# A hybrid decoder layer on one core: three blocks' probabilities turned by DMA in place of four, and the fillers placed anew

## The chip, the core and the metric

The kernel runs on one core of a Trainium2 chip. Five engines work side by side, each through its own instructions in order: TensorE (PE, matrix products into PSUM banks), VectorE (DVE), ScalarE (ACT), GpSimd (POOL) and SyncE (SP), which issues most DMA transfers. They meet through semaphores only. The metric is the device time of one execution in microseconds (us): three timed runs of the kernel before gave 1909.85 us as their median, from 1906.83 to 1912.13.

## The reference, cut to what matters

```python
def reference(x, ...):                       # x: (1, 2048, 1024) float32
    h = rms_norm(x, attn_norm_g)
    z = h @ w_in                             # 1024 -> 2304: q 512, k 128, v 128, conv B, C, X 512 each
    q, k = rms_norm(q, q_norm_g), rms_norm(k, k_norm_g)        # per head of 64; 8 heads, 2 kv heads
    y_attn = swa_sink_attention(q, k, v, sinks)                # window 128, blocks of 128, a sink per head
    y_conv = gate_b * short_conv(gate_c * xc, conv_w)          # causal, depthwise, 3 taps
    y = concatenate([rms_norm(y_attn, attn_out_g), rms_norm(y_conv, conv_out_g)])
    x = x + y @ w_out
    hm = rms_norm(x, mlp_norm_g)
    return x + square(relu(hm @ w_up)) @ w_down                # 1024 -> 4096 -> 1024
```

All inputs and outputs are float32.

## The kernel before, in words

Every large product is made of three products of two float32r parts, a high part and the rest (`mm3`, lines 288 to 290: high times high, high times low, low times high), so the weights and activations are split on ACT (a cast) and DVE (a difference).

The work has three phases. The first, the mixers, goes over the sequence in four chunks of 512 rows (`c`, 0 to 3), each of four blocks of 128 rows (`b`, 0 to 15). The second and third are the two MLP products, made by a Strassen-like scheme of seven products each (lines 1538 and 1655). The change touches the mixers alone.

In a chunk PE has two kinds of work. The large one is a list of steps that a generator (`besides`) hands out: the conv projections of this chunk (`pc`, `px`, `pb`), the conv half of the output projection (`pout`), and q, k, v of the next chunk (`pz`); in the last chunk the transposes of the rows that the MLP will need (`pt_m`, `x_blocks`) are woven in. The small one is attention, block by block, and has long chains between its products on PE: the scores (`psc`, line 786), the softmax on DVE and ACT (`sc`, the exponentials at line 803, the final product at line 811), the probabilities turned, split and masked (`pp`), the product with the values (`po`, line 891), its rounding and squares (`o`, `at`), and the sum of squares (`pa`, line 912). `fill(n)` takes `n` steps of the large list between these points. `FILL[c]` holds the counts; they set how much PE work covers each chain. `PRIO`, `PRIO_Z` and `PRIO_P` shift the priorities by which the scheduler orders the instructions on each engine, so they decide who stands ahead of whom in a queue. The order on each engine is fixed when the program is built.

Two things are turned by DMA, not on PE. From block 4 on (`TURN_Q`), q and k of a block are normed (`qk_norm`), split into two 16-bit planes in the tile `sq`, and turned by a DMA transpose (line 742). For the blocks in `TURN_P` the same is done with the probabilities: `softmax` copies each half of `sc` into planes (`half`, line 819) and starts a transpose (line 820); `values` merges the planes into `pt` (line 392). All these tiles (`sq`, `half`, `pt`) are one buffer that they take in turn. So a half can be copied only when the half before it has landed, and the norm of the next block waits for both. Other blocks' probabilities are turned by eight PE transposes (`ptp`, line 839).

The rows of the next chunk are normed, turned and split by `prepare`, a generator of nine steps. `EARLIER` says at which steps of the second pair of conv projections the first five of them are taken.

Loads of weights that were split in chunk 0 and kept in DRAM are issued on SP (line 249), in one queue with the transposes, the raw rows and the stores. An SP instruction that waits holds up all behind it.

At the end of the conv half of the output projection, `pc` sums the squares; ACT (last chunk) or DVE copies them (`ms_c`), POOL makes the reciprocal root `rc`, and DVE's line 1044 needs it to empty the banks of `pout`, of which there are three.

Of the kernel before, what the change touches and what calls it, by code (L numbers as in the profile page):

```python
# [66 lines left out]
DOWN_BUFS = {"u": 2, "x1": 7}  # L67
UP_BUFS = {"w": 17, "u2": 3, "f11": 2, "u4": 2, "f12": 2, "s1": 1, "s2": 1, "s4": 1, "st": 5}
PC = (2, 0)
TURN_P = (6, 9, 13, 15)  # L70
TURN_Q = 4
PRIO_P = ((240, 0), (120, -30), (70, -80), (0, 120))
PRIO_Z = ((-50, -120, -180), (-250, 0, 430), (210, -230, 60), (0, -50, -150))
EARLIER = (6, 14, 31, 45, 46)

CHP = CH + 32
STEPS = 3
# [9 lines left out]

PRIO = ((210, 0, 0, -70, 30, 0, 20, -10, -160, 0, 0, 310, 0, 10), (160, -60, -60, -60, 40, 50, 140, 40, 0, -90, 0, 10, 0, -120), (0, 0, 70, -10, 40, 0, 200, -40, 0, -130, 260, 150, -170, -10), (200, 0, 210, 0, 30, 0, 0, 40, -10, 0, -40, 30, 60, -120), (160, 80, 0, 10, 0, 0, 20, -20, -20, 0, 0, 120, 0, 0))  # L90

FILL = (((18, 15), (9, 8, 7, 8, 5), (5, 5, 5, 12, 9), (1, 11, 5, 9, 7), (11, 10, 8, 2, 2)), ((25, 18), (6, 14, 13, 1, 0), (19, 10, 11, 2, 3), (13, 10, 15, 7, 9), (6, 14, 8, 8, 7)), ((21, 15), (5, 22, 7, 4, 1), (8, 2, 6, 1, 9), (24, 14, 16, 0, 1), (13, 14, 9, 5, 3)), ((30, 0), (6, 8, 1, 6, 7), (11, 7, 6, 13, 6), (1, 11, 4, 7, 8), (13, 7, 7, 0, 8)))

# [1 line left out]
def hymba_layer(  # L97
# [91 lines left out]
    def ahead(i):  # L189

        offset = PRIO[stage[0]][i]
        return tc.high_priority(offset=offset) if offset else nullcontext()


    def ahead_z(i):

        offset = PRIO_Z[stage[0]][i]
        return tc.high_priority(offset=offset) if offset else nullcontext()

    def ahead_p(i):  # L200

        offset = PRIO_P[stage[0]][i]
        return tc.high_priority(offset=offset) if offset else nullcontext()
# [479 lines left out]
    with tc.tile_pool(name="mix_small", bufs=1) as mix_small, tc.tile_pool(name="mix", bufs=1) as mix:  # L683
# [90 lines left out]
        def softmax(b, qt, sc):  # L774
# [36 lines left out]
            nc.vector.tensor_tensor(sc, sc, den[:, :, None].to_broadcast([P, HEADS, P]), op=ALU.mult)  # L811
            if b in TURN_P:
                with ahead_p(0):
# [9 lines left out]
        def values(b, zt, v_before, sc, n_fill, fill):  # L823
# [3 lines left out]
            def probabilities(kv):  # L827

                if b in TURN_P:
                    pt = mix.tile([P, nh, DH], F32, tag="sq", name=f"pt_{nm}_{kv}", bufs=1)  # L830
# [228 lines left out]
        def besides(c, before, h, yt, rc, x1, h_next, z_next):  # L1059
# [8 lines left out]
            for j in range(2):  # L1068
                for n, _ in enumerate(conv_pair(c, h, j, yt, ssc)):
                    if blocks and n % X_EVERY == 0:  # L1070
                        next(blocks, None)
                    if j and not blocks and n in EARLIER:
                        next(steps)
# [41 lines left out]
        def mixers(c, before, h, z):  # L1115


            last = c + 1 == NCHUNK
            n_fill = FILL[c]
            stage[0] = c  # L1120
# [574 lines left out]
```

## Time and profile before

| what | us |
|---|---|
| timed runs: median (lowest to highest) | 1909.85 (1906.83 to 1912.13) |
| the profiled execution's own time | 1914.36 |
| its span, first to last instruction | 1912.7 |
| mixers, until the first MLP product | 690.2 |
| MLP, first product | 609.6 |
| MLP, second product and the last stores | 612.9 |

PE is busy for 1894.5 us of the span, DVE 1235.9, ACT 878.6, POOL 290.1; the mean granted clock of PE is 0.998. A row of the timeline holds the start, the length, the engine, the line, the operation, the tiles (written <- read) and shapes; in brackets stands how long the engine was idle before it and what ended that. The ends of PE's matmuls are modelled, and successive matmuls overlap: how fast PE goes is read from the starts.

### The profile page before, as it was taken

What the parts mean: (1) busy time and instruction counts of PE and PEld (TensorE: products, weight loads), DVE (VectorE), ACT (ScalarE), POOL (GpSimd) and SP (SyncE); (2) the same over time, 40 slices, a digit from 0 to 9 for tenths busy, and PEclk for the clock granted to TensorE, in tenths of its full rate; (3) what the DMA queues carried; (4) which work ended last, traced back from release to release, by engine and by line L of the source; (5) the groups of instructions that cost most, each with busy time, mean ns of one, the idle gap of its engine ahead of it and who ended that gap; (6) DMA issues with size and microseconds to landing.
All of it is one profiled execution on the core that took longest, in us unless ns stands there. A gap on an engine that the chain in (4) does not pass through costs nothing.

```text
span 1912.7 us, 24444 instructions
## 1 busy us (share of the span) xinstructions
PE 1894.5 (99%) x8742; PEld 1574.3 (82%) x8742; DVE 1235.9 (65%) x1945; ACT 878.6 (46%) x1621; POOL 290.1 (15%) x477
## 2 busy tenths in 40 slices
PE   9999999999999999999999999999999999999999
PEld 8888888888887788888888888888888888888887
DVE  5886567658558859999787766666534334448541
ACT  6665356556545446545565545454332332232320
POOL 2222213213212212233111111111000000100000
PEclk9999999999999999999999999999999999999999
DMA  8988967667687888778576544448954456866631
GB/s 297 333 285 205 332 221 227 222 216 249 210 316 228 237 303 256 221 217 249 192 241 202 175 144 159 141 147 328 361 194 151 136 172 222 284 228 213 214 128 56
DMA packets 282138, 426.13 MB, mean 223 GB/s; under 512 B 101016, under 2 KB 185760, under 8 KB 269216
## 3 DMA queue, kind: packets, MB, share of 16 engines
q1 hardware_dynamic: 253184, 348.91, 56.7%
q0 software_dynamic: 15424, 51.40, 6.9%
q10 hardware_dynamic: 13408, 24.26, 3.4%
q8 instruction: 69, 1.13, 0.3%
q14 instruction: 53, 0.43, 0.1%
HBM read 286.35 MB, written 125.83 MB: 216 GB/s over the span
## 4 chain that ended last, share of the span: by engine, by line
PE 86%; DVE 5%; DMA 4%; ACT 2%; POOL 1%; issue 1%; SPq 0%; DVEq 0%; ACTq 0%; POOLq 0%
PE u L1538 32%; PE d L1655 32%; PE pout L288 2%; PE pout L289 2%; PE pout L290 2%; PE pz L289 1%; PE pz L290 1%; PE pz L288 1%; PE pz L601 1%; DMA sc_b<-half_b 1%; PE psc_b L786 1%; PE pc_c L289 1%; PE pc_c L288 1%; PE pc_c L290 1%; PE pb_c L288 1%; PE pb_c L290 1%
## 5 line engine op out<-in xcount | busy, mean ns | idle before, releaser
L1538 PE MATMUL u<-op_x,wop 128*128 128x512 f32 x2688 | 609.8, 389 | 0.0
L1655 PE MATMUL d<-op_w,op_f 128*128 128x512 f32 x2691 | 609.5, 389 | 0.0
L1655 PEld LDWEIGHTS d<-op_w,op_f 128*128 128x128 f32 x2691 | 505.0, 188 | 104.5
L1538 PEld LDWEIGHTS u<-op_x,wop 128*128 128x128 f32 x2688 | 504.5, 188 | 105.1 <-issue 0.6
L480 DVE TENSOR_TENSOR op_f<-op_f 128x1024 fp32r<-128x1024 f32 x112 | 137.0, 1225 | 238.4 <-ACT op_f L479 237.9
L479 ACT CAST op_f<-op_f 128x1024 fp32r<-128x1024 f32 x112 | 117.7, 1051 | 354.8 <-DMA op_f<-fop 342.8
L498 ACT CAST wop<-wu 128x512 fp32r<-128x512 f32 x156 | 96.4, 620 | 91.9 <-PE u L1538 89.5
L499 DVE TENSOR_TENSOR wop<-wu,wop 128x512 fp32r<-128x512 f32 x156 | 111.0, 713 | 32.6 <-ACT wop L498 20.0
L1274 POOL DMA_DIRECT2D fop<-s x96 | 52.1, 542 | 441.3 <-DVE s L1277 434.7
L1280 DVE TENSOR_TENSOR u<-u,u 128x512 f32<-128x512 f32 x128 | 87.9, 687 | 21.3 <-PE u L1538 21.2
L480 DVE TENSOR_TENSOR op_w<-raw,op_w 128x1024 fp32r<-128x1024 f32 x56 | 68.4, 1223 | 25.1 <-ACT op_w L479 24.8
L479 ACT CAST op_w<-raw 128x1024 fp32r<-128x1024 f32 x56 | 58.8, 1051 | 44.0 <-PE d L1655 21.7
L852 POOL TENSOR_SCALAR_AFFINE_SELECT pp_b<-pp_b 128x512 fp32r<-128x512 f32 x60 | 47.7, 805 | 144.1 <-ACT pp_b L845 100.2
L1286 ACT ACTIVATE u<-u 128x512 f32<-128x512 f32 x64 | 40.4, 632 | 53.0 <-DVE u L1280 50.8
L803 ACT ACTIVATE sc_b<-sc_b,ngm_b 128x128 f32<-128x128 f32 x128 | 49.7, 390 | 20.2 <-DVE ngm_b L800 20.1
L1487 POOL DMA_DIRECT2D wds<-raw x16 | 8.5, 533 | 330.0 <-DVE raw L1485 320.1
L498 ACT CAST wop<-wu_s 128x512 fp32r<-128x512 f32 x64 | 39.5, 619 | 31.0 <-PE u L1538 27.7
L499 DVE TENSOR_TENSOR wop<-wu_s,wop 128x512 fp32r<-128x512 f32 x64 | 46.0, 720 | 11.5 <-ACT wop L498 11.3
L288 PE MATMUL pout<-w_wo,yt_c 128*128 128x512 f32 x128 | 50.5, 395 | 1.6 <-DVE x L1044 1.6
L288 PE MATMUL pb_c<-h_a,w_wb 128*128 128x512 f32 x128 | 51.8, 405 | 0.0
L290 PE MATMUL pb_c<-h_a,w_wb 128*128 128x512 f32 x128 | 51.3, 401 | 0.0
L289 PE MATMUL pb_c<-h_a,w_wb 128*128 128x512 f32 x128 | 51.3, 401 | 0.0
(253 smaller groups left out, 3144.3 us busy)
## 6 DMA issues: line engine op xcount, KB each, us to landing
op_f<-fop SPq DMA_DIRECT2D x112, 512.0 KB, 4.3
raw<-in_w_down_dram SPq DMA_DIRECT2D x72, 512.0 KB, 4.4
wu<-in_w_up_dram SPq DMA_DIRECT2D x128, 256.0 KB, 4.0
w_wo<-wo SPq DMA_DIRECT2D x24, 1024.0 KB, 6.7
fop<-s POOLq DMA_DIRECT2D x96, 256.0 KB, 2.7
fop<-u ACTq DMA_DIRECT2D x64, 256.0 KB, 2.3
op_x<-xop SPq DMA_DIRECT2D x28, 512.0 KB, 6.8
w_q<-q SPq DMA_DIRECT2D x12, 1024.0 KB, 5.7
```

Of the source, the lines that this page charges most:

```text
L288: nc.tensor.matmul(ps, st(0), mv(0), start=first, stop=False)
L289: nc.tensor.matmul(ps, st(0), mv(1), start=False, stop=False)
L290: last_sum[0] = nc.tensor.matmul(ps, st(1), mv(0), start=False, stop=last).ins
L479: nc.scalar.copy(op[:, 0], raw)
L480: nc.vector.tensor_tensor(op[:, 1], raw, op[:, 0].bitcast(F32), op=ALU.subtract)
L498: splits.append(nc.scalar.copy(hi, blk).ins)
L499: lows.append(nc.vector.tensor_tensor(lo, blk, hi.bitcast(F32), op=ALU.subtract).ins)
L803: nc.scalar.activation(sc[:, hd, :], sc[:, hd, :], AF.Exp, bias=ngm[:, hd : hd + 1], accum_out=den[:, hd : hd + 1])
L1274: eng.dma_start(fop_dram[tb][ORDER_DOWN.index(i)][n // 2][:, n % 2], b)
L1280: return nc.vector.tensor_tensor(dst, ps, b, op=ALU.add).ins
L1538: nc.tensor.matmul(pt, wops[i][:, a, k, :], xops[tb, p][k // 2][:, b, k % 2, :], start=p not in GOES_ON and k + j == 0, stop=k + j == NB + ...
L1655: nc.tensor.matmul(ps[tb][j][:, cs], fs[tb][:, a, k, j * P : (j + 1) * P], w[:, b, k, cs], start=first and p not in GOES_ON and k + n == 0 ...
```

## The change

Five tables are replaced. `TURN_P` loses block 9, whose probabilities are then turned on PE. The others say where the fillers stand, who goes first in a queue, and when the rows of the next chunk are prepared. The MLP is not edited.

```diff
-TURN_P = (6, 9, 13, 15)
+TURN_P = (6, 13, 15)
 TURN_Q = 4
-PRIO_P = ((240, 0), (120, -30), (70, -80), (0, 120))
-PRIO_Z = ((-50, -120, -180), (-250, 0, 430), (210, -230, 60), (0, -50, -150))
-EARLIER = (6, 14, 31, 45, 46)
+PRIO_P = ((-270, -750), (690, 0), (0, 0), (180, -120))
+PRIO_Z = ((-80, -60, 510), (-230, 90, 0), (130, 0, 60), (0, 0, -100))
+EARLIER = (3, 11, 32, 33, 37)
...
-PRIO = (...)
+PRIO = (...)
-FILL = (((18, 15), (9, 8, 7, 8, 5), ...
+FILL = (((18, 13), (12, 8, 7, 8, 6), ...
...
```

What moves, at three places. The first is ACT's queue in the last chunk, between the softmax of block 13 and the norm of block 14 (`half_b13` are the planes, `xt_m` raw rows that are scaled, `o_b12` the output of block 12, `sq_b14` the norm). Before:

```order
L819 COPY half_b13_0_5613<-sc_b13_5482 128x512 x2
L866 CAST vz_632<-z3_1_4875 128x2x64
L866 CAST vd_633<-v_diff_635 128x2x64
L364 ACTIVATE xt_m0_3_6161<-xt_m0_3_6161,rs_x1_233 128x1024
L364 ACTIVATE xt_m1_3_6162<-xt_m1_3_6162,rs_x1_233 128x1024
L899 COPY o_b12_5806<-po_b12_0_5737 64x512
L819 COPY half_b13_1_5617<-sc_b13_5482 128x512 x2
L866 CAST vz_632<-z3_1_4875 128x2x64
L726 ACTIVATE sq_b14_5621<-z3_2_4876 128x640
L899 COPY o_b12_5806<-po_b12_1_5801 64x512
```

and now:

```order
L819 COPY half_b13_0_5635<-sc_b13_5509 128x512 x2
L364 ACTIVATE xt_m0_3_6157<-xt_m0_3_6157,rs_x1_233 128x1024
L364 ACTIVATE xt_m1_3_6158<-xt_m1_3_6158,rs_x1_233 128x1024
L866 CAST vz_632<-z3_1_4871 128x2x64
L899 COPY o_b12_5836<-po_b12_0_5783 64x512
L866 CAST vd_633<-v_diff_635 128x2x64
L819 COPY half_b13_1_5639<-sc_b13_5509 128x512 x2
L978 CAST yt_c3_0_0_5810<-y_c3_0_0_5675 128x512
L981 ACTIVATE ssc3_5393<-y_c3_0_0_5675 128x512
L866 CAST vz_632<-z3_1_4871 128x2x64
L726 ACTIVATE sq_b14_5643<-z3_2_4872 128x640
L899 COPY o_b12_5836<-po_b12_1_5831 64x512
```

The second half of block 13 still stands behind the two raw rows and behind `o_b12`, and two conv instructions come between it and the norm of block 14.

The second is SP's queue at the end of chunk 1, where the weights of the next chunk's q are loaded (`w_q12_1` is the last of four parts). Before:

```order
L820 DMA_TRANSPOSE sc_b6_2794<-half_b6_0_2912 128x8x128
L1080 DMA x1_1_3_3049<-in_x_dram 128x1024
L430 DMA_TRANSPOSE xt_a2_3_3032<-half_a2_3_0_3118 128x8x128
L430 DMA_TRANSPOSE xt_a2_3_3032<-half_a2_3_1_3119 128x8x128
L820 DMA_TRANSPOSE sc_b6_2794<-half_b6_1_2916 128x8x128
L249 DMA w_q12_1_3363<-q1_918 128x2048
```

and now:

```order
L820 DMA_TRANSPOSE sc_b6_2794<-half_b6_0_2909 128x8x128
L1080 DMA x1_1_3_3085<-in_x_dram 128x1024
L249 DMA w_q12_1_3363<-q1_918 128x2048
L820 DMA_TRANSPOSE sc_b6_2794<-half_b6_1_2913 128x8x128
L408 DMA xt_a3_0_4285<-in_x_dram 128x1024
L430 DMA_TRANSPOSE xt_a2_3_2992<-half_a2_3_0_3155 128x8x128
L430 DMA_TRANSPOSE xt_a2_3_2992<-half_a2_3_1_3156 128x8x128
```

The load has passed three transposes.

The third is ACT's queue near the end of the last chunk, around the copy of the conv squares (`ms_c3`). Before:

```order
L866 CAST vz_632<-z3_3_4877 128x2x64
L899 COPY o_b14_6471<-po_b14_0_6423 64x512
L819 COPY half_b15_1_6281<-sc_b15_6126 128x512
L1101 COPY ms_c3_6437<-pc3_6432 128x4
L819 COPY half_b15_1_6281<-sc_b15_6126 128x512
```

and now:

```order
L899 COPY o_b14_6452<-po_b14_0_6416 64x512
L866 CAST vz_632<-z3_3_4873 128x2x64
L866 CAST vd_633<-v_diff_635 128x2x64
L983 ACTIVATE y_c3_1_1_6192<-y_c3_1_1_6192 128x512
L1101 COPY ms_c3_6433<-pc3_6428 128x4
L866 CAST vz_632<-z3_3_4873 128x2x64
L819 COPY half_b15_1_6277<-sc_b15_6122 128x512 x2
```

The copy of the squares has passed the second half of block 15.

On PE the three points that the prediction uses are: between the scores of block 13 and those of block 14 there were 126 matmuls of 512 columns and 24 transposes, and there are 126 and 36; between the scores of block 15 and its second product with the values there were 159 matmuls of 512 columns, and there are 129; between the second and third group of block 3's scores there were three, and there are eight.

More of the change, by code (lines that the diff above doesn't have):

```diff
@@ L86 @@
 SOON = 330
-PRIO = ((210, 0, 0, -70, 30, 0, 20, -10, -160, 0, 0, 310, 0, 10), (160, -60, -60, -60, 40, 50, 140, 40, 0, -90, 0, 10, 0, -120), (0, 0, 70, -10, 40, 0, 200, -40, 0, -130, 260, 150, -170, -10), (200, 0, 210, 0, 30, 0, 0, 40, -10, 0, -40, 30, 60, -120), (160, 80, 0, 10, 0, 0, 20, -20, -20, 0, 0, 120, 0, 0))
-FILL = (((18, 15), (9, 8, 7, 8, 5), (5, 5, 5, 12, 9), (1, 11, 5, 9, 7), (11, 10, 8, 2, 2)), ((25, 18), (6, 14, 13, 1, 0), (19, 10, 11, 2, 3), (13, 10, 15, 7, 9), (6, 14, 8, 8, 7)), ((21, 15), (5, 22, 7, 4, 1), (8, 2, 6, 1, 9), (24, 14, 16, 0, 1), (13, 14, 9, 5, 3)), ((30, 0), (6, 8, 1, 6, 7), (11, 7, 6, 13, 6), (1, 11, 4, 7, 8), (13, 7, 7, 0, 8)))
+PRIO = ((370, 0, -150, -100, 30, 0, -30, -10, -160, 0, 0, 480, 400, 0), (170, -60, -90, -60, 30, 110, -70, 40, 0, -80, 0, 70, 60, -140), (0, 0, 20, -10, 40, 0, 90, -40, 10, -130, 160, 60, 50, 0), (200, 0, 190, 0, 30, 0, 50, 40, 80, -30, -10, 30, 50, -90), (160, 80, 0, 10, 0, 0, 20, -20, -20, 0, 0, 120, 0, 0))
+FILL = (((18, 13), (12, 8, 7, 8, 6), (4, 2, 5, 12, 9), (1, 10, 5, 9, 10), (11, 9, 9, 2, 2)), ((25, 17), (6, 14, 13, 1, 0), (20, 10, 7, 2, 3), (12, 10, 16, 6, 12), (5, 16, 8, 5, 5)), ((16, 19), (10, 18, 5, 0, 1), (8, 2, 6, 1, 9), (28, 15, 13, 0, 6), (13, 18, 7, 7, 1)), ((30, 2), (9, 8, 1, 7, 8), (11, 3, 8, 11, 2), (2, 13, 5, 2, 6), (13, 12, 2, 0, 2)))
 @with_exitstack
```

## The prediction

> **What bounds the kernel now.** I read the page's first line, then busy time by stage, then who TensorE (PE) waited for, and last the chain of waits around the longest wait. The columns of the stages are: stretch, its length, busy us (instructions) of PE, its weight loads, DVE, ACT, POOL, granted clock, DMA share, GB/s.
>
> ```profile
> span 1912.7 us, 24444 instructions
> ...
> 140.00:300.00 160.00, 156.94 (x774) 130.00 (x773) 102.83 (x214) 84.88 (x212) 38.03 (x61) 1.00 0.82 253
> 300.00:500.00 200.00, 197.91 (x979) 166.01 (x979) 139.09 (x301) 114.94 (x279) 50.78 (x75) 1.00 0.70 228
> 500.00:690.20 190.20, 182.43 (x902) 151.49 (x902) 130.75 (x259) 85.97 (x213) 43.28 (x66) 0.98 0.77 248
> 690.20:1299.80 609.60, 609.60 (x2690) 504.54 (x2689) 478.40 (x696) 331.38 (x543) 104.72 (x168) 1.00 0.62 203
> 1299.80:1912.70 612.90, 609.32 (x2692) 504.67 (x2690) 278.71 (x270) 174.64 (x174) 22.72 (x44) 1.00 0.60 206
> ```
>
> From 690.2 us on PE never waits before the final output, and the change edits nothing there. All it can win is PE's idle time before that: 3.1 + 2.1 + 7.8 = 13.0 us in the three stretches from 140 on, and whatever the clock loses (0.98 in the last stretch). The longest waits of PE (total, times, longest):
>
> ```profile
> PE pa_b L912 <- DVE o_b L907: 3.8, 1, 3.8
> PE pz L289 <- DMA w_q<-q: 2.0, 2, 1.0
> PE pt_m L370 <- DVE xt_m L371: 2.0, 2, 1.1
> ...
> PE pout L288 <- DVE x L1044: 1.6, 1, 1.6
> ...
> PE po_b L891 <- POOL pp_b L852: 0.8, 1, 0.8
> ...
> PE psc_b L786 <- DVE sc_b L797: 0.6, 1, 0.6
> ```
>
> **The change, part by part.**
>
> *Block 9's turn goes back to PE.* Eight 128x128 transposes are added; four ACT copies, four DVE copies and two DMA transposes go, all off the path. Such transposes among matmuls, from PE's timeline (start, length):
>
> ```profile
> 549.54 0.60 PE L370 MATMUL pt_m<-ident,xt_m 128*128 128x128 f32 x4
> 549.90 0.48 PE L288 MATMUL pc_c<-h_a,w_wc 128*128 128x512 f32 x1
> 550.22 0.39 PE L289 MATMUL pc_c<-h_a,w_wc 128*128 128x512 f32 x1
> 550.45 0.39 PE L290 MATMUL pc_c<-h_a,w_wc 128*128 128x512 f32 x1
> ```
>
> A matmul of 512 columns starts 0.23 us after the one before (550.45 - 550.22). From 549.54 to 550.22 are 0.68 us, less one such matmul 0.45 for four: 0.11 each, so **+0.9** for eight. With it goes the POOL wait of 0.8, which is block 9's second product behind its DMA-turned half; transposed on PE, the probabilities have 191 matmuls of 512 columns of cover ahead of them. **-0.8** (ends: 0 and -0.8).
>
> *A weight load passes three transposes in SP's queue* (chunk 1, before the projection of chunk 2). SP's queue by time:
>
> ```profile
> 304.56 1.23 SPq L820 DMA_TRANSPOSE sc_b<-half_b  x1
> ...
> 306.55 4.59 SPq L430 DMA_TRANSPOSE xt_a<-half_a  x2
> 311.23 1.26 SPq L820 DMA_TRANSPOSE sc_b<-half_b  x1
> 312.59 0.54 SPq L249 DMA_DIRECT2D w_q<-q  x1
> ```
>
> The load at 312.59 is the one that PE waits 1.0 for at about 318. It now stands right ahead of the L430 pair at 306.55, some 6 us earlier: **-1.0**. What it pushes back is row tile a2_3 and a half of block 6, whose product has 9 score matmuls (1.1 us) more of cover. Ends: 0, if the buffer and not the queue held the load, and -1.0. Chunk 0's equal wait keeps its queue order: 0.
>
> *Scores of block 3*: eight matmuls in place of three stand between its second and third score group, 1.1 us more against a wait of 0.6: **-0.6**.
>
> *The last chunk's raw rows.* pt_m waited twice for the one bank to be emptied by DVE. Its first pair has 22 matmuls between in place of 6, and DVE now empties it before its score copies; the second pair has 9 in place of 6, 0.7 us. Of 2.0 I take **-1.5** (ends 0, -2.0).
>
> *The long wait.* The chain of waits (start, us, what) that ends at pa_b of block 12:
>
> ```profile
> 567.89 6.39 DMA xt_m<-x_dram
> ...
> 574.36 1.15 ACT xt_m L364
> ...
> 576.02 1.15 ACT half_b L819 x2
> ...
> 577.18 4.77 DMA sc_b<-half_b
> ...
> 582.04 0.75 ACT sq_b L726
> ...
> 588.80 0.21 DVE o_b L907
> ```
>
> ACT turns to block 13's second half only after a raw row tile has come in; that half's transpose frees the buffer that the norm of block 14 needs, and block 12's o_b stands behind that norm on DVE. PE pays more than the wait:
>
> ```profile
> 558.11 2.08 PE L786 MATMUL psc_b<-kw,qt_b 128*128 128x256 f32 x16
> ...
> 589.15 0.56 PE L912 MATMUL pa_b<-mean,o_b 128*128 128x1 f32 x2 [3.83 <-DVE o_b L907]
> ...
> 590.57 0.63 PE L290 MATMUL pb_c<-h_a,w_wb 128*128 128x512 f32 x1
> 591.00 0.63 PE L288 MATMUL pb_c<-h_a,w_wb 128*128 128x512 f32 x1
> ...
> 594.84 0.47 PE L288 MATMUL pc_c<-h_a,w_wc 128*128 128x512 f32 x1
> ...
> 598.56 0.64 PE L786 MATMUL psc_b<-kw,qt_b 128*128 128x256 f32 x4
> ```
>
> After 3.83 us of idleness matmuls start 0.43 apart, not 0.23, until 594.84: 12 of them, 12 x 0.20 = 2.4 us. The 1.6 us wait later on cost the clock nothing (1.00 in this stretch):
>
> ```profile
> 640.00:660.00 20.00, 18.44 (x85) 15.01 (x84) 13.09 (x24) 7.78 (x17) 5.00 (x7) 1.00 0.98 268
> ```
>
> From block 13's scores (558.11) to block 14's (598.56) are 40.4 us; the order holds 16 score matmuls there, 126 of 512 columns and 24 transposes, 16 x 0.12 (2.08 for 16, with the last one's drain) + 126 x 0.23 + 24 x 0.11 = 33.5 at PE's pace. So PE is 6.9 late by block 14, whose scores in turn start the moment their operands are there.
>
> In the changed order 12 more transposes lie between the two (+1.3 us of cover), but ACT's half of block 13 now stands behind o_b of the same block 12 whose product comes 48 matmuls and 20 transposes after the scores, 48 x 0.23 + 20 x 0.11 = 13.2 us; with the product's own four matmuls and a 64-row and a 128-column copy ahead of it (an estimate: 1.8 us) the half starts some 15.0 us after the scores, which took 16 x 0.12 = 1.9 us: 576.02 - 560.0 = 16.0 before. The chain behind is the same. Lateness 6.9 - 1.3 - 1.0 = 4.6, so **-2.3**. Its parts fall on two waits, before pa_b and before block 14's scores, 2 to 3 us each. Ends: -6.9 (transpose at its shortest and better DVE order) and 0.
>
> The Trainium skill ("TensorE: Matmul & The Clock Gate", Part 1) says the array goes to half clock after an idle window of about 3.4 us, and that this window runs free. The 0.43 after 3.83 us agrees. By it, two waits of 2 to 3 us cost no clock, and the sum stays; one joined wait of 4.6 would add the 2.4 again.
>
> *The reciprocal root of the last conv norm.* ACT's copy L1101, from ACT's and DVE's timelines:
>
> ```profile
> 648.21 0.62 ACT L819 COPY half_b<-sc_b 128x512 uint16<-128x512 uint16 x1 [2.87 <-DMA sc_b<-half_b]
> 648.85 0.16 ACT L1101 COPY ms_c<-pc 128x4 f32<-128x4 f32 x1
> 650.51 2.07 DVE L1044 SCALAR_TENSOR_TENSOR x<-pout,rc,x 128x512 f32<-128x512 f32 x3 [0.52 <-POOL rc L185]
> ```
>
> L1101 queued behind block 15's second half, which waited for the first half's transpose. It now stands ahead of it. From the copy to the first emptied bank are 2.4 us (648.85 to 650.51 plus a third of 2.07), and 12 matmuls, 2.8 us, cover it: **-1.6** (ends 0, -1.6).
>
> *What is late next: block 15.* Its second product had 159 matmuls of 512 columns behind the scores and has 129, 6.8 us less. Its scores, its last operand, its first transpose, and the landing times of all eight transposes of the kind:
>
> ```profile
> 627.07 2.15 PE L786 MATMUL psc_b<-kw,qt_b 128*128 128x256 f32 x16
> ...
> 657.35 0.69 DVE L846 TENSOR_TENSOR pp_b<-pt_b,pp_b 128x512 fp32r<-128x512 f32 x1
> ...
> 639.81 8.37 DMA sc_b<-half_b
> ...
> DMA to landing us min/median/max: 2.7/2.9/8.4
> ```
>
> Here, with 8.37 for the first, the operand was there 658.0 - 629.1 = 29 us after the scores; 129 matmuls, 12 transposes and 6 short ones are some 31.4: 2.4 to spare. With 8.37 for the second too, in place of 2.9, it is 5.5 later, 3.1 short. I take **+1.0** between 0 and 3.1, for this and for smaller covers that shrank.
>
> Sum: 0.9 - 0.8 - 1.0 - 0.6 - 1.5 - 2.3 - 1.6 + 1.0 = **-5.9**. The profiled execution took 1914.36 us, 1.7 around its span; it becomes 1908.5. It is 4.5 above the median of the runs shown, 1909.85, so I set the difference against that: **1904**.
>
> **Rivals.**
>
> *A. The chain hides entirely.* If block 13's second transpose lands in the median 2.9 and not 4.77, 1.9 less; with DVE's better order (block 14's copy no longer behind a conv product, 1.5) the lateness is near 1. With block 15 safe too: 1904 - 3.4 - 1.0 = 1899.6. For it: half of the eight landed within 2.9. Against: ACT's half still sits behind a load.
>
> *B. The long wait belongs to the profiled execution.* That execution is 4.5 slower than the median; if late transfers made the 3.83 and the 1.6, the timed runs hold less to win: -5.9 + 2.3 + 1.6 leaves -2.0, 1908. Against: the waits of 0.6 to 1.1 are in queue order, not in lateness.
>
> *C. Late transposes decide.* The place is ACT in the last chunk, where both remaining DMA-turned blocks have their halves behind other work. At 8.37 in place of 4.77 block 13 is 3.6 later; the joined wait passes 3.8 and costs the clock 2.4; block 15 is short by 3.1, and its wait, between the 1.6 after which the clock stayed at 1.00 and the 3.83 that cost 2.4, adds 1.2. 1904 - 1.0 + 3.6 + 2.4 + 3.1 + 1.2 = 1913, slower than before. It decides from about 5 us of landing time for block 13 and 5.3 for block 15's second. For it: both blocks had a late one. Against: the one at 639.81 ran beside weight loads that are now issued in another order.
>
> *D. Nothing moves*, because each wait only shifts to the next consumer: 1909.85 + 0.9 = 1911.
>
> **How the numbers follow.** Forecast 1904: 0.36. A: 0.25. B: 0.18. C: 0.11. D: 0.10. What a measurement of this kernel can tell from no change is about 0.3%, 5.7 us: faster means under 1904.1. That takes half of the forecast and all of A, and a little of B: 0.46. Slower, above 1915.6, takes C's worse side and a tail of unforeseen waits: 0.10. Same: 0.44. The range 1895 to 1913 takes in A with its unknown ends (the many waits of 0.2 to 0.4 that I cost at nothing) and D, and reaches to C.
>
> **What would show it.** Right: the wait of pa_b under 3 us with the clock at 1.00 from 580 to 600; no w_q wait near 318; no wait of pout for L1044 near 650; PE's MLP start at 683 to 685 in place of 690.2. Wrong: a wait of po_b in the last chunk, block 14's scores waiting over 3 us, or PE idle again over 10 us after 140.

## The result and the profile after

The changed kernel takes 1915.63 us (median; 1912.38 to 1918.11) against 1910.65 (1906.44 to 1913.57) for the kernel before on the same chip. The ratio is 1.0026 [1.0018, 1.0034]: **5 us slower**, where 5.9 faster was forecast, and outside the range of 1895 to 1913.

The stages again, with the columns of before:

```profile
span 1913.5 us, 24453 instructions
...
140.00:300.00 160.00, 156.23 (x774) 129.77 (x773) 101.98 (x211) 84.45 (x207) 38.98 (x60) 1.00 0.80 253
300.00:500.00 200.00, 197.31 (x966) 165.10 (x965) 140.62 (x297) 113.62 (x279) 48.41 (x74) 0.99 0.70 228
500.00:690.20 190.20, 184.67 (x923) 153.46 (x923) 131.30 (x261) 87.44 (x215) 43.66 (x67) 0.99 0.77 246
690.20:1299.80 609.60, 609.60 (x2691) 504.55 (x2690) 477.87 (x696) 331.04 (x542) 105.03 (x168) 1.00 0.62 203
```

PE's idle time after 140 us is 3.8 + 2.7 + 5.5 = 12.0 us where it was 13.0. By this pair of profiles the kernels look alike: 1915.2 us in the profiled execution of the changed kernel, 1914.36 in that of the kernel before. But the first is at the median of its timed runs and the second 3.7 above its own. PE's waits in the changed kernel (total, times, longest):

```profile
PE pa_b L912 <- DVE vd L867: 4.1, 1, 4.1
PE pz L289 <- DMA w_q<-q: 1.8, 1, 1.8
...
PE po_b L891 <- DVE pp_b L846: 1.5, 2, 1.0
PE pc L1093 <- DVE ssc L984: 1.4, 1, 1.4
PE pa_b L912 <- DVE o_b L907: 1.2, 1, 1.2
PE psc_b L786 <- DVE kw L768: 0.9, 1, 0.9
PE pt_m L370 <- DVE xt_m L371: 0.5, 1, 0.5
```

Four waits of before have gone or shrunk as forecast: w_q near 318 us, block 3's scores, pt_m (2.0 to 0.5), pout for L1044 in the last chunk (1.6 to none). The long wait, of pa_b for block 12, is longer (3.8 to 4.1; its row names `vd`, the last instruction of DVE to end before it, but `pa_b` reads `o_b`, which was ready 0.15 us earlier). And three stand where nothing was forecast: pa_b of block 3 (1.2), pc of chunk 2 (1.4), and w_q between chunks 0 and 1, which was 1.0 and is 1.8. Two smaller ones were not forecast either: block 7's scores wait 0.9 for `kw`, and block 13's product with the values waits 1.0 in the last chunk, where it waited 0.4.

**Chunk by chunk over all profiles.** One profile of each kernel can't carry a difference of 5 us whose terms are 1 us each. The runs below built kernels that share whole chunks with one kernel or the other, so each chunk's order was profiled four to ten times. A stage ends with the first matmul of the q projection of the next chunk, so the stage called chunk 2's below also holds the end of chunk 1, from block 7's scores on. In the changed kernel these marks are, and the first MLP product behind them:

```profile
148.80 0.48 PE L288 MATMUL pz<-w_q,h_a 128*128 128x512 f32 x1
...
315.11 0.39 PE L288 MATMUL pz<-w_q,h_a 128*128 128x512 f32 x1
...
486.15 0.39 PE L288 MATMUL pz<-w_q,h_a 128*128 128x512 f32 x1
...
690.95 0.61 PE L1538 MATMUL u<-op_x,wop 128*128 128x512 f32 x2
```

| stage, us | order of before: mean (lowest to highest, profiles) | changed order | difference |
|---|---|---|---|
| to pz of chunk 1 | 147.9 (147.6 to 148.4, 10) | 148.7 (148.3 to 149.1, 6) | +0.8 |
| to pz of chunk 2 | 165.2 (164.0 to 167.2, 10) | 166.4 (165.7 to 167.6, 6) | +1.2 |
| to pz of chunk 3 | 166.8 (166.2 to 167.5, 9) | 170.2 (169.5 to 171.0, 5) | +3.4 |
| to the first MLP product | 205.3 (203.2 to 208.2, 6) | 206.0 (204.8 to 207.6, 4) | +0.7 |
| MLP, to PE's last matmul | 1219.4 (1218.8 to 1221.3, 12) | 1218.9 (1218.8 to 1219.1, 5) | -0.5 |

The sum, +5.6, agrees with the timed +5.0. The last two differences are smaller than the spread of the profiles, so they show nothing. Two things are seen that the one profile of before hid. The loss is in chunks 0 to 2, above all in chunk 2 (to pz of chunk 3). And the profile on which the prediction stood has the longest last chunk of its six, 208.2 us: nearly 3 us above their mean.

The +3.4 of chunk 2 can be taken apart over the same profiles. PE's idle time there rises by 1.0 us (mean 1.3 and 2.3). In three of the five changed profiles the granted clock is 0.5 for 3.4 us, in none of the nine before: 1.0 us on the mean. And PE makes 32 transposes there, not 20: eight are block 9's, and four are made here and no longer in the last chunk. At the 0.11 us each of the prediction that is 1.3 us, of which the four only moved.

### The profile page after: what moved, and what is told of

Read it like the earlier page. It is cut to its first block, busy times and chain, and to the rows that moved or that the text cites. A ratio compares the mean times of both kernels' runs of the same rounds, so it can differ in the third digit from the quotient of the medians.

```text
span 1913.5 us, 24453 instructions
## 1 busy us (share of the span) xinstructions
PE 1895.9 (99%) x8750; PEld 1574.7 (82%) x8750; DVE 1236.4 (65%) x1941; ACT 877.1 (46%) x1617; POOL 290.6 (15%) x477
## 4 chain that ended last, share of the span: by engine, by line
PE 89%; DVE 5%; DMA 3%; ACT 1%; issue 1%; POOL 0%; SPq 0%; DVEq 0%; ACTq 0%; POOLq 0%
PE u L1538 32%; PE d L1655 32%; PE pout L288 2%; PE pout L289 2%; PE pout L290 2%; PE pz L289 1%; PE pz L288 1%; PE pz L290 1%; PE pc_c L289 1%; PE pc_c L290 1%; PE pc_c L288 1%; PE px_c L290 1%; PE px_c L289 1%; PE px_c L288 1%; PE pz L601 1%; PE psc_b L786 1%
## 5 line engine op out<-in xcount | busy, mean ns | idle before, releaser
L498 ACT CAST wop<-wu_s 128x512 fp32r<-128x512 f32 x64 | 39.4, 620 | 30.2 <-PE u L1538 26.2
L290 PE MATMUL pc_c<-h_a,w_wc 128*128 128x512 f32 x128 | 51.1, 399 | 0.0
L289 PE MATMUL pc_c<-h_a,w_wc 128*128 128x512 f32 x128 | 51.0, 399 | 0.0
L288 PE MATMUL pc_c<-h_a,w_wc 128*128 128x512 f32 x128 | 51.0, 399 | 0.0
```

The lines of the kernel that those rows point to most:

```text
L288: nc.tensor.matmul(ps, st(0), mv(0), start=first, stop=False)
L289: nc.tensor.matmul(ps, st(0), mv(1), start=False, stop=False)
L290: last_sum[0] = nc.tensor.matmul(ps, st(1), mv(0), start=False, stop=last).ins
L498: splits.append(nc.scalar.copy(hi, blk).ins)
```

## The experiments

All kernels here compute the whole reference. Tables that an edit does not name are those of the kernel that it starts from.

**1 to 3. The change chunk by chunk.** The kernel before, with the changed rows of the tables for some chunks.

```diff
 e1  +PRIO, PRIO_Z, PRIO_P, FILL of chunks 0 and 1; EARLIER
 e2  +PRIO, PRIO_Z, PRIO_P, FILL of chunk 2; TURN_P = (6, 13, 15)
 e3  +PRIO, PRIO_Z, PRIO_P, FILL of chunk 3
```

Chunks 0 and 1:

> The kernel before, with the change's tables for chunks 0 and 1 alone (and its times of row preparation); all four blocks turned by DMA, chunks 2 and 3 as before. Theory 'last chunk' (block 13's halves copied late behind raw rows, and a transpose of 7.37 us: the loss of 5 us is made in chunk 3): nothing is lost here, and the wait of 1.0 us for the load of w_q near 318 us goes: -1 us, 0.999 to 1.000 of before. Theory 'chunk 2' (the loss is made where pc waits 1.35 us for DVE and PE then runs cold for seven us): -1 us here too. Theory 'transfers' (the three moved groups each push some transfers later, so that the loss is spread): +1.5 us, near 1.001.

Chunk 2:

> The kernel before, with the change's tables for chunk 2 alone and block 9 turned on PE. Theory 'last chunk': 0 us, 1.000. Theory 'chunk 2': the wait of pc, the cold stretch near 465 us and eight transposes, less the POOL wait of block 9: 1.35 + 1.6 + 0.9 - 0.8 = +3 us, 1.0016. Theory 'transfers': +1.5 us, 1.001.

Chunk 3:

> The kernel before, with the change's tables for chunk 3 alone. Theory 'last chunk': the whole loss, +5 us, 1.0026, with a wait of pa_b for block 12 of 3 us or more and the matmuls after it 0.43 us apart. Theory 'chunk 2': -2 us, 0.999, since the waits of pt_m and of pout for L1044 are gone and the long wait is no longer than before. Theory 'transfers': +2 us, 1.001.

Measured: 1.0008 [0.9999, 1.0016], 1.0008 [0.9999, 1.0017], 1.0000 [0.9991, 1.0009]. The theory that all 5 us are made in the last chunk falls: its tables alone cost nothing, though its profile has the wait of pa_b at 5.1 us. The first two point to a loss spread over chunks 0 to 2, but neither interval excludes no change, and the sum is 1.0016. The first run's profile has the same new waits in the same places as the changed kernel's, so they belong to the order (pa_b's 4.5 is 1.2 for block 3 and 3.4 for block 12):

```profile
PE pa_b L912 <- DVE o_b L907: 4.5, 2, 3.4
...
PE pz L289 <- DMA w_q<-q: 1.4, 1, 1.4
```

**4. Block 13 turned on PE, in the kernel before.**

```diff
-TURN_P = (6, 9, 13, 15)
+TURN_P = (6, 9, 15)
```

> The kernel before, with block 13's probabilities turned on PE (eight transposes more), all else the same. If the long wait of pa_b for block 12 (3.83 us, and 2.4 us of slow clock after it) is there in every execution and comes from block 13's late transposes, it goes: -6.2 + 0.9 = -5 us, 0.997. If it belonged to the one profiled execution, there is nothing to win: 0 to +1 us, 1.000 to 1.0005. In both cases the profile shows no wait of pa_b for block 12 over 2 us.

Measured: 0.9995 [0.9987, 1.0004]. The wait of pa_b for block 12 is gone from the profile, and 2.5 us for pout has come in chunk 3's start: freed of block 13's planes, the norms of blocks 14 and 15 run early on DVE, wait there for POOL, and the row updates L1044 queue behind them. So neither theory holds: the wait was no chance of one execution (all six profiles of the order before have it, 0.9 to 3.8), but the gain went to the next queue.

**5. The changed kernel again.**

> The changed kernel once more, unchanged: another execution of the same order. Theory 'order' (the new waits are in the queues' order and come back in every execution): 1.0025, +5 us; pc of chunk 2 waits 1.3 us again, pa_b of block 3 1.2 us, pa_b of block 12 3 us or more. Theory 'lateness' (the waits of the first profile were one execution's late transfers): at least two of the three are under 0.5 us. Whether the matmuls after pc are again 0.43 us apart tells if the slow clock there belongs to the order or to chance.

Measured: 1.0024 [1.0011, 1.0037]; pc of chunk 2 waits 1.36, pa_b of block 3 1.27, pa_b of block 12 3.34. The waits are the order's. The granted clock behind pc was 0.5 again for 3.4 us, some 1.7 us lost, as in the first profile.

**6. Two of the new waits taken away.**

```diff
-PRIO[0][6] = -30
+PRIO[0][6] = 20
...
-                    if (i, j) == PC:
+                    if (i, j) == ((PC[0], 2) if c == 2 else PC):
```

> The changed kernel with two of its new waits taken away: pc of chunk 2 stands two steps (six matmuls, 1.4 us) later, and the shift PRIO of chunk 0 for the outputs of the values is 20 again, so that ACT takes block 3's first output copy ahead of the last weight splits. Theory 'order': 1.35 + 1.2 = 2.6 us less than the changed kernel, 4 us less where the clock went with the wait: 1.0005 to 1.0012. Theory 'they only move' (the next consumer waits instead): no less than the changed kernel, 1.0025.

Measured: 1.0054 [1.0042, 1.0066], over 5 us slower still. PE's waits:

```profile
PE pa_b L912 <- DVE vd L867: 5.2, 1, 5.2
PE pz L289 <- DMA w_q<-q: 2.9, 1, 2.9
PE pa_b L912 <- DVE o_b L907: 2.6, 1, 2.6
PE pout L288 <- DVE x L1044: 2.5, 1, 2.5
```

pc no longer waits, and pout waits 2.5 for L1044 in its place: the chain from the sum of squares to the emptied bank was late, and a later pc cannot shorten it. The shift for block 3 made its wait 2.6 in place of 1.2. Stage 2 is 170.3 us, as in the changed kernel; stage 1 is 171.0, 4.6 longer. A wait is not removed where PE stands, but where the late operand is made.

**7 and 8. Block 13 on PE, and the norms kept back.** e7 is the changed kernel, e8 the one before, both with:

```diff
-TURN_P = (6, 13, 15)          # e7; in e8 (6, 9, 13, 15)
+TURN_P = (6, 15)              # e7; in e8 (6, 9, 15)
...
+            done[b] = nc.vector.tensor_tensor(
                 sc, sc, den[:, :, None].to_broadcast([P, HEADS, P]), op=ALU.mult
+            ).ins
...
-                    with ahead(2):
-                        qk_norm(c * NT + t + 1, z[t + 1])
+                    b = c * NT + t
+                    with ahead(2), tc.issue_after(done[b - 1]) if b > 12 else nullcontext():
+                        qk_norm(b + 1, z[t + 1])
```

> The changed kernel with block 13's probabilities turned on PE, and the norms of blocks 14 and 15 issued on DVE behind the softmax of blocks 12 and 13 (else they come too early, as in the run with block 13 on PE before). The wait of pa_b for block 12 (4.1 us) and the slow clock after it (1.6 us) go, eight transposes come: 4.8 us less than the changed kernel, 1.000. If PE meets another wait in their place: 1.002.

> The kernel before, block 13 turned on PE, with the norms of blocks 14 and 15 issued on DVE behind the softmax of blocks 12 and 13. In the first run with block 13 on PE these norms stood among the row updates L1044 ahead of block 12, which PE waited 0.8 and 2.5 us for, with 1.6 us of slow clock behind. With these gone: 1908.96 - 4.9 = 1904 us, 0.9970. If they only make room for the next wait: 0.9995 as in that run.

Measured: e7 1.0022 [1.0012, 1.0031], e8 0.9990 [0.9980, 0.9999]. In e7 the last stage is 203.9 us in place of 206.0, but the stages before keep what they lose; 1.000 was too much. In e8 the new wait is again DVE waiting for POOL. Now block 13's score copies (L799) queue behind it, and they empty a bank that the second four transposes of block 12 need (DVE, then PE):

```profile
562.75 0.83 DVE L731 TENSOR_TENSOR z<-z,rq_b 128x640 f32<-128x640 f32 x1 [2.07 <-POOL rq_b L185]
...
563.93 0.30 PE L843 MATMUL ptp_b<-ident,sc_b 128*128 128x128 f32 x1 [1.69 <-DVE sc_b L799]
```

**9 and 10. What of chunk 2 is the turn, what the tables.**

```diff
 e9   +TURN_P = (6, 13, 15), all else as before
 e10  +PRIO, PRIO_Z, PRIO_P, FILL of chunk 2; TURN_P as before
```

> The kernel before, with block 9 turned on PE and nothing else edited. In the built order of this kernel DVE takes seven or eight merges of the next chunk's rows (L392) ahead of the last sum of the conv squares (L984), where the kernel before takes one. Theory 'the turn itself makes chunk 2 late': +0.6 us from the first projection of block 8 to the conv half, and a wait of pc for L984 of 0.5 to 1.4 us: 1.0005 to 1.0010, and from pz of chunk 2 to pz of chunk 3 168 to 169 us (before: 166 to 167.5). Theory 'the fillers and priorities make it late': the transposes alone, no wait of pc over 0.3 us, 1.0003.

> The kernel before, with the change's tables for chunk 2, and block 9 still turned by DMA. Theory 'the turn itself makes chunk 2 late': no wait of pc over 0.3 us, 1.0000. Theory 'the fillers and priorities make it late': pc waits 1.0 us or more, 169 us from pz of chunk 2 to pz of chunk 3, 1.0008 to 1.0013.

Measured: 0.9995 [0.9987, 1.0004] and 1.0005 [0.9995, 1.0015]. The times don't tell the two apart; the profiles do in part. Chunk 2's stage is 168.1 us with the turn alone and 169.9 with the tables alone (before 166.8, both 170.2), and pc waits 0.7 in each, 1.4 with both. So both theories are half right: each brings about half of pc's wait, and the tables the greater share of the stage. Some of that share is e10's own: from block 8's scores to the conv half it takes 82.2 us where the changed order takes 81.0, since PE comes late through block 9's product with the values, whose DMA-turned halves it waits for. The full changed chunk 2 has the last sum of squares (L984) on DVE 5.3 us later after the kernel's start than the chunk as before (e3), 2.6 of which it brings along from chunks 0 and 1 (its first matmul at 315.1 and 312.5). The rest is in two steps. The last matmul of projection pb, its first reader on DVE (L975), the last sum of squares, and pc; the changed kernel, then e3:

```profile
457.24 0.39 PE L290 MATMUL pb_c<-h_a,w_wb 128*128 128x512 f32 x1
460.04 0.69 DVE L975 TENSOR_TENSOR y_c<-pb_c,y_c 128x512 f32<-128x512 f32 x1
...
463.00 0.68 DVE L984 TENSOR_TENSOR ssc<-ssc,y_c 128x512 f32<-128x512 f32 x1
```

```profile
453.38 0.40 PE L290 MATMUL pb_c<-h_a,w_wb 128*128 128x512 f32 x1
454.54 0.69 DVE L975 TENSOR_TENSOR y_c<-pb_c,y_c 128x512 f32<-128x512 f32 x1
...
457.67 0.69 DVE L984 TENSOR_TENSOR ssc<-ssc,y_c 128x512 f32<-128x512 f32 x1
458.41 1.05 PE L1093 MATMUL pc<-mean,ssc 128*128 128x1 f32 x8
```

PE starts the matmul 3.9 us later, and DVE takes its result 2.8 us after that start in place of 1.2. pc had no margin in the order before: it starts as L984 ends (458.41 and 458.36), so DVE's 1.6 are a wait of 1.4. In DVE's queue all eight merges (L392) of the next chunk's first two row tiles and one split (L445) now stand ahead of L984; in the order before two merges did, and six and all the splits came behind it. That these merges are the whole of the delay was not tried, and their number alone does not settle it: e9 has all eight ahead of L984 and e10 three, and pc waits 0.7 in both.

**11 and 12. The load of w_q.**

```diff
-with tc.high_priority(offset=100) if name == "wo11" and c + 1 == NCHUNK else nullcontext():
+with tc.high_priority(offset=150 if name == "q1" else 100) if name == "q1" or name == "wo11" and c + 1 == NCHUNK else nullcontext():
```

e11 is the changed kernel with this edit, e12 is e8 with it.

> The changed kernel, with the loads of the second half of w_q put 150 earlier: in chunk 0 the last one stands ahead of the pair of row transposes L430 on SP, not behind it. In five profiles PE waited 1.4, 1.8, 1.9, 2.2 and 2.9 us for it in orders made from the change's chunk 0, and 0, 0, 0, 0.6 and 1.0 in those made from the tables before. If that place in SP's queue is the cause: the wait is under 0.3 us, and 1.5 to 2 us less than the changed kernel, 1.0016. If the load waits for its buffer: as the changed kernel, 1.0025, with the row transposes later.

> The kernel before with block 13 turned on PE, the norms of blocks 14 and 15 behind the softmax of blocks 12 and 13, and the w_q loads earlier as well: 1909.3 - 1.1 - 0.5 (the two waits for w_q in the run without it) = 1907.7, 0.9982. If the load waits for its buffer, no gain: 0.9990.

Measured: 1.0056 [1.0043, 1.0068] and 1.0000 [0.9992, 1.0009]. The wait for w_q is gone from both profiles, so the place in the queue was its cause; the load did not wait for a buffer. But e11 is slower by 6 us than the changed kernel, and e12 by 2 than e8; the 2 are not clear of the intervals. In e11 w_qkv, whose load the row transposes passed, is waited for at once (0.9). In chunk 1 the load of w_q passed one row load, but SP's order of loads and of q and k transposes behind it changed as well, and block 7's products wait for three engines:

```profile
PE po_b L891 <- POOL pp_b L852: 1.9, 2, 1.7
...
PE po_b L891 <- DVE pp_b L846: 1.6, 3, 0.7
PE po_b L891 <- ACT pp_b L845: 1.5, 1, 1.5
```

In e12 w_qkv is waited for 1.1 in w_q's place. By the stages 4.2 of the 6 us of e11 lie between pz of chunk 2 and pz of chunk 3 (174.4 us in place of 170.2), where block 7's products are and where PE is idle for 6.7 us in place of 2.3. How much each transfer makes was not tried.

**13 and 14. The norm in two parts.** On top of e8, the part of the norm that needs POOL's root is issued on DVE behind the row maxima of the block before, so DVE has work while POOL makes it. e14 turns block 9 on PE too.

```diff
-        def qk_norm(b, zt):
+        def qk_norm(b, zt, after=None):
...
+            with tc.issue_after(after) if after else nullcontext():
                 nc.vector.tensor_tensor(zqk, zqk, rq[:, :, None].to_broadcast([P, nh, DH]), op=ALU.mult)
...
-            nc.vector.tensor_reduce(ngm, sc, axis=AX.X, op=ALU.max, negate=True)
+            top[b] = nc.vector.tensor_reduce(ngm, sc, axis=AX.X, op=ALU.max, negate=True).ins
...
-                        qk_norm(b + 1, z[t + 1])
+                        qk_norm(b + 1, z[t + 1], top[b] if b > 12 else None)
```

> The kernel before with block 13 turned on PE. In the run before of this kind the second part of the norms of blocks 14 and 15 waited on DVE for POOL's reciprocal root (2.1 and 1.9 us), with block 13's scores and the raw rows' banks queued behind, and PE waited 1.7 and 1.6 us for those. Here that part stands behind the row maxima of blocks 13 and 14. If those waits go: 1909.3 - 3.3 = 1906 us, 0.9973. If they only move to block 14's scores, whose operands are then 2 us later: 0.9990.

> As the run above, with block 9 turned on PE as well, so that only blocks 6 and 15 are turned by DMA. By the run with block 9 alone on PE (0.9995) it adds -1 us to it: 0.9968. If chunk 2's pc then waits for L984 as in the changed kernel (0.65 us there): the same as the run above, 0.9973.

Measured: 1905.39 us, 0.9977 [0.9958, 0.9996], and 1906.66 us, 0.9976 [0.9965, 0.9987]: **both beat the two kernels**, by about 4.5 us the one before and about 9.5 the changed one. That is near what was expected (0.9973 and 0.9968); the turn of block 9 adds nothing that can be seen. What is shown is the gain of the edits together: block 13 on PE, the norms kept back and the norm in two parts. The last of them alone, against e8 (0.9990 [0.9980, 0.9999]), is not clear of the intervals. The last stage of e14, with the columns as above:

```profile
500.00:690.20 190.20, 187.23 (x941) 156.30 (x940) 129.16 (x257) 85.58 (x212) 43.65 (x76) 1.00 0.76 259
```

PE is idle 3.0 us there, 7.8 before and 5.5 in the changed kernel, and the clock is 1.00.

**15 and 16. Chunk 2 given back; the row preparation alone.**

```diff
 e15 (changed kernel)  -PRIO, PRIO_Z, PRIO_P, FILL of chunk 2, TURN_P
                       +the same of the kernel before
 e16 (kernel before)   -EARLIER = (6, 14, 31, 45, 46)
                       +EARLIER = (3, 11, 32, 33, 37)
```

> The changed kernel with the tables of chunk 2 of the kernel before, and block 9 turned by DMA. By the stages, chunk 2 (from its q projection to that of chunk 3) takes 170.2 us in three profiles of the changed order and 166.9 in five of the one before: 3.3 us less than the changed kernel, 1.0008, with 166 to 168 us for this stage. If the loss in chunk 2 comes from how chunks 0 and 1 leave the queues, the stage stays at 169 us or more, 1.0025.

> The kernel before with the changed times of row preparation (EARLIER) alone. If these make the wait for w_q between chunks 0 and 1 (1.4 to 2.2 us in the changed order, 0 to 1.0 in the one before, with SP's queue in one order): a wait of 1.4 us or more there, and 1.0005 to 1.0010. If the fillers and priorities of chunk 0 make it: a wait under 1 us, 1.0000.

Measured: 1.0009 [1.0000, 1.0018] and 0.9998 [0.9989, 1.0008]. e15 is the clearest run of all: chunk 2's stage falls to 480.86 - 314.53 = 166.3 us and the time by some 3 us, to 1.0009 where 1.0008 was expected. Its marks:

```profile
314.53 0.39 PE L288 MATMUL pz<-w_q,h_a 128*128 128x512 f32 x1
...
480.86 0.48 PE L288 MATMUL pz<-w_q,h_a 128*128 128x512 f32 x1
```

So some three fifths of the loss (3.4 of 5.6 by stages) are chunk 2's own, not what chunks 0 and 1 leave behind. The same tables put alone into the kernel before (e2) cost less by the timed runs, 1.5 us, with an interval from 0 to 3. The row preparation alone costs nothing that can be measured. With it w_q waits 0.9, within the 0 to 2.0 of the order before, so the longer wait of the changed order (mean 1.7) is put down to chunk 0's fillers and priorities by exclusion; they were not run alone.

**17. Why block 13 is late.** In the changed order SP issues a weight load 0.5 us ahead of block 13's first transpose, in the order before behind it. SP's queue before, then in the changed kernel:

```profile
572.86 1.28 SPq L820 DMA_TRANSPOSE sc_b<-half_b  x1
574.19 0.57 SPq L249 DMA_DIRECT2D w_wx<-wx  x1
```

```profile
576.21 0.32 SPq L249 DMA_DIRECT2D w_wx<-wx  x1
576.74 1.27 SPq L820 DMA_TRANSPOSE sc_b<-half_b  x1
```

In the kernel before, that transpose landed after 2.8 us, in the changed kernel after 7.4. The same split is in every profile with block 13 turned by DMA: 2.8 in four, 3.4 and 5.2 with the load behind, 5.0 to 9.6 in six with the load ahead. In e17 both loads of w_wx go behind the second transpose.

```diff
-            with tc.high_priority(offset=100) if name == "wo11" and c + 1 == NCHUNK else nullcontext():
+            soon = tc.high_priority(offset=100) if name == "wo11" and c + 1 == NCHUNK else nullcontext()
+            with soon, tc.issue_after(flipped[13]) if name == "wx1" and c + 1 == NCHUNK else nullcontext():
...
-                        nc.sync.dma_start_transpose(half.rearrange("p (n t) -> p n t", t=P), planes)
+                        flipped[b] = nc.sync.dma_start_transpose(half.rearrange("p (n t) -> p n t", t=P), planes).ins
```

> The changed kernel, with the two loads of w_wx issued on SP behind block 13's second transpose (in the changed order the first of them stands right ahead of the first transpose, in the order before right behind it). In the profiles of the changed chunk 3 that first transpose took 7.4, 5.0, 8.1 and 8.6 us to land. Theory 'the load ahead of it delays the transpose': it lands in under 3.5 us, pa_b of block 12 waits under 1.5 us (4.1, 3.3, 5.1, 5.4 before), and the slow clock after it goes: 4 us less than the changed kernel, 1.0005. Theory 'the transpose is slow for another reason (stores, the other row loads)': it still takes 5 us or more, 1.0025.

Measured: 1.0026 [1.0016, 1.0035]: no gain, and yet half of the theory is shown. The chain of waits in the changed kernel, and in e17 (start, us, what):

```profile
564.85 1.91 PE psc_b L786 x16
...
576.74 7.37 DMA sc_b<-half_b
584.19 1.15 ACT half_b L819 x2
585.36 4.47 DMA sc_b<-half_b
589.91 0.75 ACT sq_b L726
...
597.62 0.35 PE pa_b L912 x2
```

```profile
577.08 2.79 DMA sc_b<-half_b
...
581.12 3.02 DMA sc_b<-half_b
584.22 0.75 ACT sq_b L727
...
590.61 1.35 ACT sq_b L742 x2
591.99 0.59 ACT o_b L900
...
596.36 0.56 PE pa_b L913 x2
```

The transposes land in 2.8 and 3.0 us in place of 7.4 and 4.5, and block 14's norm starts 5.7 us earlier. But now ACT makes that norm's planes (L742) ahead of the second copy of block 12's output (L900, 591.99), DVE's o_b is done only at 596.2, and pa_b still waits 3.3 us. PE gets there 1.3 us sooner, and nothing is left of that at the MLP (691.5 and 691.0): in this profile the half clock around that wait lasted 6.8 us, in the changed kernel's 3.4. Behind the norm DVE waits for POOL's reciprocal root once more (1.9 us in e17, 1.8 in the changed kernel), with block 12's output queued behind. The slow transpose was a cause of the lateness, not what bounded the time.

**18. The changed chunk 3, with block 13 on PE and the norms in two parts**, in the kernel before.

```diff
 e13 +PRIO, PRIO_Z, PRIO_P, FILL of chunk 3
```

> The kernel before with the change's tables for chunk 3, block 13 on PE, and the second part of the norms of blocks 14 and 15 behind the row maxima. The change's chunk 3 takes waits of pt_m away (1.5 us in the run with the tables before) and should then be worth that: from chunk 3's q projection to the MLP 201.5 us in place of 202.8, 1904 us, 0.9965. If these waits move on: 0.9977, as with the tables before.

Measured: 0.9983 [0.9974, 0.9992]. The last stage is 203.3 us, not 201.5: pt_m, which waits 0.5 in the changed kernel, waits 2.5 at one place here. These waits too move on.

## Why the prediction was wrong

Taken by its own terms, with means over the profiles that share the order (six of the last chunk before, four changed; ten and six of chunks 0 and 1, nine and five of chunk 2; unless said otherwise):

| term | forecast | measured | |
|---|---|---|---|
| block 9's eight transposes, and the POOL wait of its product | +0.9 - 0.8 | +0.3 | from block 8's scores to the conv half 81.0 us (6 profiles with block 9 on PE), 80.7 (8 by DMA); the wait was 0 to 0.8 |
| w_q near 318 | -1.0 | -0.8 | right: 0.2 to 1.2 before, none after |
| scores of block 3 | -0.6 | -0.6 | right, in every profile |
| pt_m | -1.5 | -1.3 | right: 1.8 to 0.5 |
| pout for L1044 | -1.6 | -0.3 | 1.6 in the one profile, 0.5 in another, none in four |
| long wait of block 12 | -2.3 | +1.7 | mean 2.8 before, 4.5 changed (3.3 to 5.4); wrong sign |
| block 15's product and smaller covers | +1.0 | +0.5 | block 15's product waited in none; block 13's waited 0.3 before, 0.9 changed |
| pa_b of block 3 | none | +1.2 | 1.2 in all six changed, none before |
| w_q between chunks 0 and 1 | 0 | +1.2 | 0.5 before (0 to 2.0), 1.7 changed (1.3 to 2.2) |
| w_qkv, the next load behind it | none | -0.4 | 0.7 before, 0.3 changed |
| block 7's scores, for kw | none | +0.5 | 0.1 before, 0.6 changed (0 to 1.1) |
| pc of chunk 2 | none | +1.4, and 1.0 of half clock on the mean | none before; 1.7 of half clock in three of five changed |

The measured column adds up to +4.4, of 5.0 by the timed runs.

**The step that decided is one that was not made.** The prediction costed the places where PE already waited, and put chunks 0 to 2 beyond their three named waits at nothing, without naming the work that would hide what else moved. But nearly every count and priority there was replaced too. These stages became longer by 0.8, 1.2 and 3.4 us, and e15 shows that the largest part is made by chunk 2's own tables. There DVE finishes the conv sum late: pc's wait of 1.4 and the half clock behind it make 2.4. That a queue keeps its order ("chunk 0's equal wait keeps its queue order: 0") says nothing of when the entries ahead become ready.

**Two terms were sized by one execution.** The profile of before was 4.5 above the median of three runs (3.7 above that of the sixteen), and the prediction saw that; it set the difference against the median and kept the terms. But its excess sat in the very chunk from which 4.4 of the 5.9 were to come (1.5, 2.3 and 1.6, less the 1.0). The 1.6 for pout was one execution's (rival B, right in this point); the long wait was in every profile, from 0.9 to 3.8.

**The long wait** failed where rival C said it could: the transposes landed late (7.4 and 4.5 us in the changed profile). The prediction took ACT's second half of block 13 to start 15.0 us behind that block's scores, 16.0 before, with the same chain behind ("The chain behind is the same"); it started 17.4 behind (584.19 less 564.85 + 1.91), since it waited for the first transpose. That is the step that failed: the chain was not the same. In SP's queue a load of w_wx had passed block 13's first transpose, a move that is not among the three places that the prediction goes by, and the transpose landed in 7.4 us in place of 2.8. From block 13's scores to block 14's the mean went from 39.4 us to 42.1, of which 1.3 are the 12 transposes more; and the lateness fell on the one wait before pa_b, not on two, since block 14's scores did not wait. C priced this at 1913 and gave it 0.11, by block 13 and block 15 together; block 15 was in time. e17 shows that even with prompt transposes the wait stays 3.3 us, since the next queue on ACT takes their place. So C named the right link and not the bound.

Rival D, that each wait only shifts to the next consumer, describes best what the runs show, in seven of them (4, 6, 8, 11, 12, 17, 18). It put the sum at +1; the consumers next in line cost more than the waits removed.

The forecast named signs of being wrong: a wait of po_b in the last chunk, block 14's scores waiting over 3 us, or PE idle over 10 us after 140. The first came (1.0, for block 13) and the third (12.0); block 14's scores did not wait. Of the signs of being right, the waits of w_q near 318 and of pout for L1044 near 650 went, but pa_b waited 4.1 where under 3 was said, with the clock at 0.5 behind it, and the MLP started at 691.0, not at 683 to 685.

## What to carry to other kernels

In this kernel, whose bounding engine is 99% busy, a wait of 1 us is the tail of a chain through several queues. Removing it where it is seen moved it in seven runs. What helped was to take the DMA turn of block 13 out of the chain and, by the profiles, to take the work that waits for a slow engine off the head of a queue that others stand in (the norm in two parts): the last stage's idle time is 4.6 us in e8 and 2.8 and 2.9 in e13 and e14. Where every table is replaced, go through every queue in which order changed, not only those where the bounding engine waited; and size the terms from several executions if there are any, above all when the one profile is above the median.

## What was not expected of the hardware

**The clock after a wait of 1.4 us.** The prediction took it that waits of 2 to 3 us cost no clock. pc of chunk 2 waits 1.35 to 1.37 us in five profiles, followed by eight one-column matmuls of 0.9 us together. Three times the granted clock was then 0.5 for 3.4 us, some 1.7 us lost; twice nothing. The changed kernel, and e2 with the same wait:

```profile
463.74 1.05 PE L1093 MATMUL pc<-mean,ssc 128*128 128x1 f32 x8 [1.35 <-DVE ssc L984]
...
465.45 0.63 PE L290 MATMUL pout<-w_wo,yt_c 128*128 128x512 f32 x1
465.88 3.15 PE L786 MATMUL psc_b<-kw,qt_b 128*128 128x256 f32 x16
```

```profile
460.83 1.05 PE L1093 MATMUL pc<-mean,ssc 128*128 128x1 f32 x8 [1.37 <-DVE ssc L984]
...
462.52 2.07 PE L786 MATMUL psc_b<-kw,qt_b 128*128 128x256 f32 x16
```

Over all profiles after 100 us, each of the 10 waits from 3.3 us up went with half clock, for 3.4 or 6.8 us; of the 12 waits from 2.0 to 2.9, nine did, for 3.4 us, and three did not. Of the 34 waits from 1.0 to 2.0 that did not stand before pc, none did. But of the nine waits of pc, 0.7 to 1.6 us long, four did, the shortest 0.96 (e13), while the longest (1.62, e11) did not. So the length of the wait alone does not decide, and what sets pc apart is the eight one-column matmuls behind it. That these count as idle would fit, since a wait of 0.96 and their 0.9 together are close to 2 us; no run varies them alone. That the same wait costs the clock in one execution and not in the next agrees with what the Trainium skill says ("TensorE: Matmul & The Clock Gate", Part 1), that the window of activity runs free. That a wait of 1.35 us with weak matmuls behind it can be enough is not in what the Trainium skill says there of an idle window of about 3.4 us; the measurement decides.

**The landing of a transpose.** Block 13's first transpose landed in 7.4, 5.0, 8.1 and 8.6 us where a weight load of one megabyte had been issued up to 1.3 us ahead of it, and in 7.7 and 9.6 in e11 and e6, which stand in the same order. With the load 1.3 us behind, as in the kernel before, it landed in 2.8 us in four profiles, in 3.4 and in 5.2 in the others. The two orders differ in other transfers too; only e17 moves the load alone, with 2.8, and its edit moved a few instructions on ACT as well. So the profile of before had a transpose of each kind on show: block 13's first, load behind, 2.8 us, and block 15's first, with a load issued 0.4 us ahead, 8.4.
